# Loading the state-space decay rows on GpSimd's queue, with the first pair of each group taken out of the chain of side pieces

## The chip, the cores and the metric

The kernel runs on one core of a Trainium2 chip. The metric is the device time of one execution in microseconds (us), lower is better; several executions are taken and their median is compared. The engines are TensorE (PE, matmuls), VectorE (DVE), ScalarE (ACT), GpSimd (POOL) and SyncE (SP, which here only issues DMAs).

## The reference

One layer of a hybrid decoder trunk over 512 tokens of width 1024, in float32. A modulated RMSNorm gives h; one projection of h feeds three branches, whose gated sum goes through an output projection, and an MLP follows. The branch that the change touches is the state-space one (16 heads of 64 in two groups, chunks of 128 tokens). Cut to what matters:

```python
h = _rms(x, norm1_w) * (1 + sc1) + sh1
z, xbc, dt_raw, q, k, v, u, gates = split(h @ w_in)
xbc = silu(causal_dwconv(xbc, conv_w, conv_b))          # xs, B, C
a_cum = cumsum((dt * A) per chunk)
decay = exp(where(causal, a_cum[l] - a_cum[s], -inf))   # 128x128 per chunk and head
cb = einsum('bclgn,bcsgn->bclsg', C, B)
y_diag = einsum('bclgsj,bcsgjp->bclgjp', cb * decay, X) # X = xs * dt
states = einsum(B, X * exp(a_cum[last] - a_cum));  prev = scan over the chunks
y = y_diag + (C . prev) * exp(a_cum) + D * xs
y = rms_per_group(y * silu(z)) * ssd_norm_w;   y_ssd = y @ w_ssd_out
y_attn = dilated window attention @ w_attn_out
y_pool = (multi-scale pooling of u, mixed) @ w_pool_out
x = x + g1 * ((g_ssd*y_ssd + g_attn*y_attn + g_pool*y_pool) @ w_out)
x = x + g2 * (square(relu(h2 @ w_ff1)) @ w_ff2)         # h2: second modulated norm
```

## The kernel before

All activations lie with channels on 128 partitions and the 512 tokens along the row. Each float32 product is made of three matmuls over a high and a low part (mm3: lines L294, L295 and L296 of the profile are its three calls). A generator, wstream, streams weights: for each pair of 128-row blocks SyncE loads a 512 KB tile raw, ScalarE copies it to the high part wh (L279), VectorE subtracts for the low part wl (L280), and 24 matmuls follow. gemm_feat runs such a stream of 4 pairs into four PSUM banks psacc.

PSUM has 8 banks, and SBUF has 49 slots of 128x512 that all small tensors share (blk). Both are handed out first in, first out: a tensor takes the slot that was freed longest ago, whatever it held. So the first matmul into a new accumulator waits for the last reader of the tensor that had that bank before; and a load waits in the same way for the last user of its slot.

The state-space branch is side work. It is cut into pieces that wait in a list, side; after every weight pair tick() runs the next piece, and after every second one also a background piece that dots a 512-wide row block of the adaLN weights on VectorE (wa, L246, with its load). A scheduler then orders the instructions of each engine. The order of pieces for a group g of 8 heads is written in the main sequence: ssd_states(g) (transposes, cb L870, X L882, states, prev L895 and L897/L898), then do_heads(g), which drives four generators ssd_heads(g, j), one for each pair of heads:

- stage 1 loads two rows of prow, broadcast to 128 partitions, as the tiles M (256 KB each);
- stage 2 makes e = exp(-M) (ACT L917), relu(M - a) in four blocks on VectorE (L924) or ScalarE (L922), exp (ACT L925) and the product with cb (DVE L926);
- stage 3 does the matmuls psy (L932) and psyo (L940), adds them to conv (L935, L941, L943) and multiplies by z (L946).

Piece j of do_heads runs stage 1 of pair j+2, stage 2 of pair j+1 and stage 3 of pair j. ssd_scale and ssd_norm (psrr, diag L221, L959, split L322) follow. The main sequence around them is: x and z of group 0 (GEMMs xs0, z0), of group 1 (xs1, z1), then the gates and projections of the attention branch (GA0, its projection, GA1, its projection, in which L751 multiplies the projection by the gate sg), two pooling GEMMs U0 and U1 (windows L976 to L982 on VectorE, then four pooling mixes, psmix, whose weights wmix are split by L279 and L280 too and whose results are written by L1000), and the gate GS0 of the state-space branch.

Of the kernel before, what the change touches and what calls it, by code (L numbers as in the profile page):

```python
# [17 lines left out]
P = 128  # L18
D = 1024
T = 512  # L20
# [78 lines left out]
def kernel(ctx: ExitStack, tc: tile.TileContext, a: dict, out: bass.AP, dbg=None):  # L99
    nc = tc.nc  # L100
# [16 lines left out]
    class Slots:  # L117
# [12 lines left out]
        def free(self, t):  # L130
            self.idle.append(self.used.pop(id(t))[0])
# [3 lines left out]
    def blk(name, dt=F32):  # L135
        return sb.take(name, dt)
# [15 lines left out]
    def psm(name="m"):  # L152
        return banks.take("ps" + name, F32)
# [4 lines left out]
    def show(name, ap):  # L158
        if dbg is not None:
            dbg(name, ap)  # L160
# [64 lines left out]
    def add_square(sums, x):  # L225
        if sums is None:
            sums = blk("sums")
            S.activation(sums, x, AF.Square)
        else:
            sq = blk("sq")  # L230
            S.activation(sq, x, AF.Square)
            V.tensor_tensor(sums, sums, sq, ALU.add)
            free(sq)
        return sums
# [26 lines left out]
    side, ticks = [], [0]  # L261
# [508 lines left out]
    st = {}  # L770
# [132 lines left out]

    def ssd_heads(g, j, xs, z):

        X, prev, cb, CT = st[g]
        pc, npc, prow = st["pc"], st["npc"], st["prow"]

        Ms = [blk("M") for _ in range(2)]
        for half in range(2):  # L910
            hd = g * 8 + 2 * j + half
            nc.sync.dma_start(Ms[half], prow[hd : hd + 1, :].broadcast_to([P, T]))
        yield
        e = blk("e")
        for half in range(2):
            hd, M, fs = g * 8 + 2 * j + half, Ms[half], slice(64 * half, 64 * half + 64)
            S.activation(e[fs, P:], M[fs, P:], AF.Exp, scale=-1.0)  # L917
            for c in range(4):
                cs = slice(c * P, (c + 1) * P)
                hc = slice(c * 16 + hd, c * 16 + hd + 1)  # L920
                if half:
                    S.activation(M[:, cs], M[:, cs], AF.Relu, bias=npc[:, hc])  # L922
                else:
                    V.tensor_scalar(M[:, cs], M[:, cs], pc[:, hc], 0.0, ALU.subtract, ALU.max)  # L924
            S.activation(M, M, AF.Exp, scale=-1.0)  # L925
            V.tensor_tensor(M, M, cb, ALU.mult)  # L926
        yield
        yp = psm("y")
        for c in range(4):
            cs = slice(c * P, (c + 1) * P)  # L930
            for half in range(2):
                mm(yp[half * 64 : half * 64 + 64, cs], lhsT=X[c][:, (2 * j + half) * 64 : (2 * j + half + 1) * 64], rhs=Ms[half][:, cs], start=True, stop=True)  # L932
        free(*Ms)
        y = xs[j]
        V.scalar_tensor_tensor(y, xs[j], dcol[:, 4 * g + j : 4 * g + j + 1], yp, ALU.mult, ALU.add)  # L935
        free(yp)
        op = psm("yo")
        for c in range(3):
            cs = slice((c + 1) * P, (c + 2) * P)
            mm(op[:, cs], lhsT=prev[c][:, j * P : (j + 1) * P], rhs=CT[:, cs], start=True, stop=True)  # L940
        V.tensor_tensor(e[:, P:], op[:, P:], e[:, P:], ALU.mult)  # L941
        free(op)
        V.tensor_tensor(y[:, P:], y[:, P:], e[:, P:], ALU.add)  # L943
        show(f"y{g}{j}", y)
        free(e)
        V.tensor_tensor(y, y, z[j], ALU.mult)  # L946
        free(z[j])
        if j == 3:
            free(*X, *prev, cb, CT)
        st["sums", g] = add_square(st.get(("sums", g)), y)  # L950
# [66 lines left out]
    def call(f, *args):  # L1017
        side.append(lambda: f(*args))
# [22 lines left out]
    def rest(n):  # L1041
        side.extend([lambda: None] * n)

    def do_heads(g, xs, z):

        gens = [ssd_heads(g, j, xs, z) for j in range(4)]
        side.append(lambda: next(gens[0]))
        for j in range(-1, 4):
            def go(j=j):
                for i in (j + 2, j + 1, j):  # L1050
                    if 0 <= i < 4:
                        next(gens[i], None)
            side.append(go)
        rest(1)
        call(ssd_scale, g)
        call(ssd_norm, g, xs)
# [29 lines left out]
    do(ssd_states(0, xs0, BC), 6)  # L1086
    z0 = take_z(0)
    do_heads(0, xs0, z0)
    xs1 = take_x(1)
    z1 = take_z(1)  # L1090
    do(ssd_states(1, xs1, BC), 6)
    sg = gate(GA, 0)
    do_heads(1, xs1, z1)
    project(a["w_attn_out"], 4, 0, oh, ol, sg, first=True)
    sg = gate(GA, 1)
# [388 lines left out]
```

## Time and the profile before

| | before |
|---|---|
| median of 3 runs | 1095.87 us (1095.17 to 1096.69) |
| profiled execution, its own time | 1098.25 us |
| its span in the trace | 1096.5 us |
| TensorE busy | 1087.1 us |
| VectorE busy | 717.4 us |
| ScalarE busy | 527.8 us |
| GpSimd busy | 3.6 us |
| granted TensorE clock | 1.00 |

The span is the time from the first to the last instruction of the trace; the execution's own time is 1.75 us longer. Rows below show start and duration in us from the span's start, and in square brackets how long the engine stood idle just before, and what ended that.

### The profile page before, as it was taken

To read this page: it belongs to the slowest core of one execution; us is meant where nothing else is said; L and a number is where in the kernel's file an instruction comes from. 1 tells how busy PE (TensorE), PEld (TensorE's weight loads), DVE (VectorE), ACT (ScalarE), POOL (GpSimd) and SP (SyncE) were. 2 spreads that over 40 slices of the span, in tenths; PEclk is the share of its full clock that TensorE was granted. 3 is DMA by queue.
4 is the path that set the end of the run, shared out by engine and by line. 5 is a ranking of instruction groups with operands and counts; after the bars stand their busy time and mean duration, and the time that the engine had idled before them with its cause. 6 is when DMAs were issued, how large, how long until landed. Compare 5 with 4: busy or idle time off the path is not lost.

```text
span 1096.5 us, 14976 instructions
## 1 busy us (share of the span) xinstructions
PE 1087.1 (99%) x5806; PEld 927.0 (85%) x5806; DVE 717.4 (65%) x1383; ACT 527.8 (48%) x845; POOL 3.6 (0%) x10
## 2 busy tenths in 40 slices
PE   9999999999999999999999999999999999999998
PEld 7878888888887877888888888899889989989987
DVE  8975874582776778568843424577787587686664
ACT  8965875543695536625432123354344334335330
POOL 0000000000000000000000000000000000000000
PEclk9999999999999999999999999999999999999999
DMA  9853342443542354321232325360214224134032
GB/s 349 306 183 98 128 134 86 152 168 102 173 125 87 117 181 136 104 97 58 96 115 97 106 96 163 97 230 1 79 57 154 65 90 136 59 114 135 20 116 77
DMA packets 46666, 133.98 MB, mean 122 GB/s; under 512 B 5362, under 2 KB 6130, under 8 KB 46596
## 3 DMA queue, kind: packets, MB, share of 16 engines
q1 hardware_dynamic: 45392, 130.28, 36.0%
q0 software_dynamic: 480, 1.57, 0.5%
q10 hardware_dynamic: 724, 1.18, 0.3%
q8 instruction: 45, 0.74, 0.3%
q14 instruction: 25, 0.20, 0.1%
HBM read 130.89 MB, written 2.13 MB: 121 GB/s over the span
## 4 chain that ended last, share of the span: by engine, by line
PE 87%; ACT 4%; DVE 3%; DMA 3%; issue 1%; SPq 0%; ACTq 0%; DVEq 0%
PE psacc L294 22%; PE psacc L296 22%; PE psacc L295 22%; PE psacc L1345 11%; PE psacc L534 4%; DMA M<-prow 2%; PE psS L613 1%; DMA wa<-in_w_ada_dram 1%; DVE conv L850 1%; ACT wh L279 1%; PE pso L729 1%; PE pso L727 1%; DVE wl L280 1%; PE pskT L597 0%; PE psqT L592 0%
## 5 line engine op out<-in xcount | busy, mean ns | idle before, releaser
L280 DVE TENSOR_TENSOR wl<-raw,wh 128x1024 fp32r<-128x1024 f32 x140 | 171.0, 1222 | 192.2 <-ACT wh L279 190.9
L279 ACT CAST wh<-raw 128x1024 fp32r<-128x1024 f32 x140 | 146.8, 1050 | 241.1 <-PE psacc L295 168.8
L294 PE MATMUL psacc<-hl,wh 128*128 128x512 f32 x416 | 166.6, 401 | 3.4 <-DVE X L882 2.2
L295 PE MATMUL psacc<-hh,wh 128*128 128x512 f32 x416 | 162.1, 390 | 0.0
L296 PE MATMUL psacc<-hh,wl 128*128 128x512 f32 x416 | 162.0, 390 | 0.0
L295 PE MATMUL psacc<-ah,wh 128*128 128x512 f32 (+1 forms) x260 | 100.4, 386 | 0.0
L294 PE MATMUL psacc<-al,wh 128*128 128x512 f32 (+1 forms) x260 | 100.4, 386 | 0.0
L296 PE MATMUL psacc<-ah,wl 128*128 128x512 f32 (+1 forms) x260 | 100.3, 386 | 0.0
L294 PEld LDWEIGHTS psacc<-hl,wh 128*128 128x128 f32 x416 | 78.2, 188 | 21.7 <-DVE X L882 2.7
L295 PEld LDWEIGHTS psacc<-hh,wh 128*128 128x128 f32 x416 | 78.2, 188 | 16.9 <-issue 1.4
L296 PEld LDWEIGHTS psacc<-hh,wl 128*128 128x128 f32 x416 | 78.1, 188 | 16.7
L294 PE MATMUL psacc<-wl,rh 128*128 128x512 f32 x192 | 76.9, 401 | 0.0
L296 PE MATMUL psacc<-wh,rl 128*128 128x512 f32 x192 | 75.5, 393 | 0.0
L295 PE MATMUL psacc<-wh,rh 128*128 128x512 f32 x192 | 75.3, 392 | 0.0
L296 PEld LDWEIGHTS psacc<-ah,wl 128*128 128x128 f32 x260 | 48.8, 188 | 9.9
L294 PEld LDWEIGHTS psacc<-al,wh 128*128 128x128 f32 x260 | 48.9, 188 | 9.7
L295 PEld LDWEIGHTS psacc<-ah,wh 128*128 128x128 f32 x260 | 48.9, 188 | 9.6
L1405 DVE SCALAR_TENSOR_TENSOR xr<-psacc,modv,xr 128x512 f32<-128x512 f32 (+1 forms) x65 | 44.7, 739 | 18.6 <-PE psacc L296 18.6
L246 DVE SCALAR_TENSOR_TENSOR wa<-wa,crow 128x512 f32<-128x512 f32 x64 | 43.1, 688 | 20.0 <-DMA wa<-in_w_ada_dram 20.0
L296 PEld LDWEIGHTS psacc<-wh,rl 128*128 128x128 f32 x192 | 36.0, 188 | 7.6
L294 PEld LDWEIGHTS psacc<-wl,rh 128*128 128x128 f32 x192 | 36.1, 188 | 7.3 <-ACT qT L593 0.2
L295 PEld LDWEIGHTS psacc<-wh,rh 128*128 128x128 f32 x192 | 36.1, 188 | 7.0
(408 smaller groups left out, 2360.8 us busy)
## 6 DMA issues: line engine op xcount, KB each, us to landing
raw<-in_w_in_dram SPq DMA_DIRECT2D x80, 512.0 KB, 3.5
raw<-in_w_ff_dram SPq DMA_DIRECT2D x52, 512.0 KB, 3.7
wa<-in_w_ada_dram SPq DMA_DIRECT2D x64, 256.0 KB, 3.6
wada<-in_w_ada_dram SPq DMA_DIRECT2D x14, 512.0 KB, 7.8
rawl<-in_w_ff_dram SPq DMA_DIRECT2D x12, 512.0 KB, 3.5
wst<-in_w_in_dram SPq DMA_DIRECT2D x16, 256.0 KB, 7.8
M<-prow SPq DMA_DIRECT2D x16, 256.0 KB, 3.8
raw<-in_w_ssd_out_dram SPq DMA_DIRECT2D x8, 512.0 KB, 3.5
```

The source lines that it names most:

```text
L246: V.scalar_tensor_tensor(wa[i], wa[i], 1.0, crow[i], ALU.mult, ALU.mult, accum_out=d[:, i : i + 1])
L279: S.copy(wh, raw)
L280: V.tensor_tensor(wl, raw, wh.bitcast(F32), ALU.subtract)
L294: mm(ps, lhsT=wh, rhs=xl, start=first, stop=False)
L295: mm(ps, lhsT=wh, rhs=xh, start=False, stop=False)
L296: mm(ps, lhsT=wl, rhs=xh, start=False, stop=last)
L534: mm(ps[j], lhsT=t[:, j, :], rhs=w, start=first, stop=last)
L613: mm(so[b], lhsT=qT[:, b * P : (b + 1) * P], rhs=kT[:, (b + 1) * P - n : (b + 1) * P], start=True, stop=True)
L727: mm(od, lhsT=vs[kb][:, hs], rhs=pT[b // 2][:, cs : cs + P], start=(b == 0), stop=False, skip_group_check=True)
L729: mm(ov[:, b, :], lhsT=vs[b][:, hs], rhs=pT[0][:, b * P : (b + 1) * P], start=False, stop=(gi == 2 and b == 3), skip_group_check=True)
L1345: mm(o, lhsT=x[:, cs], rhs=y, start=first and k == 0 and j == 0 and n == 0, stop=k == 3 and n == 2, skip_group_check=True)
L1405: V.scalar_tensor_tensor(xT[d][:, ts], p[:, : ts.stop - ts.start], modv[:, 3, d : d + 1], xT[d][:, ts], ALU.mult, ALU.add)
```

## The change

The two loads of M go to GpSimd's queue, the look-up of the group's states moves behind the first yield, and do_heads makes the loads of the first pair at once instead of as a side piece of its own.

```diff
     def ssd_heads(g, j, xs, z):
 
-        X, prev, cb, CT = st[g]
         pc, npc, prow = st["pc"], st["npc"], st["prow"]
 
         Ms = [blk("M") for _ in range(2)]
         for half in range(2):
             hd = g * 8 + 2 * j + half
-            nc.sync.dma_start(Ms[half], prow[hd : hd + 1, :].broadcast_to([P, T]))
+            nc.gpsimd.dma_start(Ms[half], prow[hd : hd + 1, :].broadcast_to([P, T]))
         yield
+        X, prev, cb, CT = st[g]
         e = blk("e")
...
         gens = [ssd_heads(g, j, xs, z) for j in range(4)]
-        side.append(lambda: next(gens[0]))
+        next(gens[0])
         for j in range(-1, 4):
```

Each engine keeps its work, but much of it changes place. Numbers at the end of a name tell one tensor from another and differ between the two kernels.

VectorE at the beginning of the gate GA0. wl are weight splits, conv_3013, conv_3019 and conv_3025 the outputs of head pairs 1, 2 and 3 of group 0, wa the adaLN dots. Before:

```order
L246 SCALAR_TENSOR_TENSOR wa_3905,dot_3909<-wa_3905,crow_81 128x512
L246 SCALAR_TENSOR_TENSOR wa_3906,dot_3909<-wa_3906,crow_81 128x512
L248 TENSOR_TENSOR modv_94<-dot_3909 128x1
L280 TENSOR_TENSOR wl_3798<-raw_3795,wh_3797 128x1024
L935 SCALAR_TENSOR_TENSOR conv_3019<-conv_3019,dcol_93,psy_3665 128x512
L941 TENSOR_TENSOR e_3585<-psyo_3675,e_3585 128x384
```

Now:

```order
L246 SCALAR_TENSOR_TENSOR wa_3920,dot_3923<-wa_3920,crow_81 128x512
L946 TENSOR_TENSOR conv_3019<-conv_3019,z_3211 128x512
L248 TENSOR_TENSOR modv_94<-dot_3923 128x1
L256 TENSOR_TENSOR modv_94<-modv_94,vec_79 128x1
L232 TENSOR_TENSOR sums_3510<-sums_3510,sq_3652 128x512
L924 TENSOR_SCALAR M_4268<-M_4268,pc_947 128x128
L280 TENSOR_TENSOR wl_3815<-raw_3812,wh_3814 128x1024
L935 SCALAR_TENSOR_TENSOR conv_3025<-conv_3025,dcol_93,psy_3685 128x512
L941 TENSOR_TENSOR e_3620<-psyo_3695,e_3620 128x384
```

Head pair 3 stands where pair 2 stood, and an L924 on an M row of group 1 has moved ahead of the weight split and of L935.

VectorE from cb of group 1 to the X that a bank of the gate GA1 waits for. Before:

```order
L870 TENSOR_TENSOR cb_3957<-pscb_3964,cst 128x512
L924 TENSOR_SCALAR M_4245<-M_4245,pc_947 128x128
L926 TENSOR_TENSOR M_4413<-M_4413,cb_3957 128x512
L924 TENSOR_SCALAR M_4279<-M_4279,pc_947 128x128
L924 TENSOR_SCALAR M_4245<-M_4245,pc_947 128x128 x2
L751 TENSOR_TENSOR sg_3914<-psacc_3922,sg_3914 128x512
L751 TENSOR_TENSOR sg_3915<-psacc_3923,sg_3915 128x512
L751 TENSOR_TENSOR sg_3916<-psacc_3924,sg_3916 128x512
L751 TENSOR_TENSOR sg_3917<-psacc_3925,sg_3917 128x512
L882 TENSOR_TENSOR X_4005<-psX_4000,dt_885 128x512
```

Now, the last twelve rows of this stretch (ahead of them stand cb, two wa products, two splits L322, four L926 and a tiny one):

```order
L882 TENSOR_TENSOR X_3979<-psX_3974,dt_885 128x512
L280 TENSOR_TENSOR wl_4090<-raw_4087,wh_4089 128x1024
L887 TENSOR_TENSOR Xd_3981<-X_3979,dst_950 128x512
L256 TENSOR_TENSOR modv_94<-modv_94,vec_79 128x1
L926 TENSOR_TENSOR M_4268<-M_4268,cb_3906 128x512
L246 SCALAR_TENSOR_TENSOR wa_4376,dot_4379<-wa_4376,crow_81 128x512
L751 TENSOR_TENSOR sg_3928<-psacc_3940,sg_3928 128x512
L751 TENSOR_TENSOR sg_3929<-psacc_3941,sg_3929 128x512
L751 TENSOR_TENSOR sg_3930<-psacc_3942,sg_3930 128x512
L751 TENSOR_TENSOR sg_3931<-psacc_3943,sg_3931 128x512
L280 TENSOR_TENSOR wl_4141<-raw_4138,wh_4140 128x1024
L897 TENSOR_TENSOR prev_4084<-prev_4024,dec_949 128x512
```

The next row is L882 of X_4018, which the bank waits for. The L924 on freshly loaded rows have left the stretch (they run earlier), and X of the first chunk stands a whole weight pair earlier.

VectorE in the gate GS0, around the split of a mixing weight wmix. Before:

```order
L976 COPY win_4868<-win_4865 128x2
L977 TENSOR_TENSOR win_4868<-win_4865 128x510
L981 TENSOR_TENSOR win_4856<-win_4856,cst 128x15
L280 TENSOR_TENSOR wl_4950<-wmix_4947,wh_4949 128x512
L280 TENSOR_TENSOR wl_4978<-raw_4975,wh_4977 128x1024
```

Now:

```order
L976 COPY win_4902<-win_4899 128x8
L977 TENSOR_TENSOR win_4902<-win_4899 128x504
L981 TENSOR_TENSOR win_4884<-win_4884,cst 128x15
L280 TENSOR_TENSOR wl_4948<-wmix_4945,wh_4947 128x512
L280 TENSOR_TENSOR wl_4976<-raw_4973,wh_4975 128x1024
```

The split that stood here belonged to mix 0 and now belongs to mix 1 (mix 0 is done at the end of U1). Ahead of it the windows of U1 have gone further (win_4902 at 8 tokens where win_4868 stood at 2), and two L1000 of mix 0 stand among them.

## Rows read from the trace of the kernel before

**Rows 1.** The page: span, and busy us (share) of each engine.

```profile
span 1096.5 us, 14976 instructions
...
PE 1087.1 (99%) x5806; PEld 927.0 (85%) x5806; DVE 717.4 (65%) x1383; ACT 527.8 (48%) x845; POOL 3.6 (0%) x10
```

**Rows 2.** Waits of TensorE: who for whom, total us, times, longest.

```profile
PE psacc L294 <- DVE X L882: 2.2, 1, 2.2
...
PE psacc L294 <- DVE conv L935: 0.5, 1, 0.5
PE psacc L294 <- ACT prev L895: 0.5, 1, 0.5
```

**Rows 3.** TensorE's timeline at three places: start, us, instruction, idle before.

```profile
336.81 0.50 PE L294 MATMUL psacc<-hl,wh 128*128 128x512 f32 x1 [0.50 <-ACT prev L895]
...
388.90 0.50 PE L294 MATMUL psacc<-hl,wh 128*128 128x512 f32 x1 [0.51 <-DVE conv L935]
...
431.01 0.50 PE L294 MATMUL psacc<-hl,wh 128*128 128x512 f32 x1 [2.22 <-DVE X L882]
431.35 0.40 PE L295 MATMUL psacc<-hh,wh 128*128 128x512 f32 x1
431.58 0.39 PE L296 MATMUL psacc<-hh,wl 128*128 128x512 f32 x1
```

**Rows 4.** VectorE's timeline ahead of the third place.

```profile
422.34 0.68 DVE L870 TENSOR_TENSOR cb<-pscb,cst 128x512 f32<-128x512 f32 x1
...
427.29 0.68 DVE L924 TENSOR_SCALAR M<-M,pc 128x128 f32<-128x128 f32 x3 [2.92 <-DMA M<-prow]
427.88 2.48 DVE L751 TENSOR_TENSOR sg<-psacc,sg 128x512 f32<-128x512 f32 x4
430.27 0.68 DVE L882 TENSOR_TENSOR X<-psX,dt 128x512 f32<-128x512 f32 x1
```

**Rows 5.** The chain that ended last, in order of time: start, us, link.

```profile
311.42 3.30 DMA M<-prow
...
420.13 3.87 DMA M<-prow
```

**Rows 6.** SyncE's timeline: DMA issues ahead of the third place.

```profile
419.53 2.20 SPq L912 DMA_DIRECT2D M<-prow  x3
```

**Rows 7.** The page's DMA issues: engine, count, KB each, median us to landing.

```profile
M<-prow SPq DMA_DIRECT2D x16, 256.0 KB, 3.8
...
al<-in_const_dram POOLq DMA_DIRECT2D x4, 256.0 KB, 3.3
...
toNat<-in_const_dram POOLq DMA_DIRECT2D x1, 256.0 KB, 4.2
toMod<-in_const_dram POOLq DMA_DIRECT2D x1, 256.0 KB, 4.3
```

**Rows 8.** Tile al, last line of its view.

```profile
DMA to landing us min/median/max: 2.9/3.3/4.7
```

**Rows 9.** Tile M, last line of its view.

```profile
DMA to landing us min/median/max: 3.1/3.8/6.5
```

**Rows 10.** VectorE's timeline at the start of GA0 (starts give the pitch).

```profile
386.96 1.23 DVE L280 TENSOR_TENSOR wl<-raw,wh 128x1024 fp32r<-128x1024 f32 x1
388.10 0.74 DVE L935 SCALAR_TENSOR_TENSOR conv<-conv,dcol,psy 128x512 f32<-128x512 f32 x1
388.76 0.55 DVE L941 TENSOR_TENSOR e<-psyo,e 128x384 f32<-128x384 f32 x1
```

**Rows 11.** VectorE's timeline in GS0: windows, then a weight split.

```profile
527.70 0.15 DVE L976 COPY win<-u 128x1 f32<-128x1 f32 x1
527.76 0.68 DVE L977 TENSOR_TENSOR win<-u 128x511 f32<-128x511 f32 x1
528.36 0.68 DVE L322 TENSOR_TENSOR pdl<-win,pdh 128x512 fp32r<-128x512 f32 x1
...
530.38 0.69 DVE L280 TENSOR_TENSOR wl<-wmix,wh 128x512 fp32r<-128x512 f32 x1
```

## Prediction

> **What bounds the kernel now.** I read the page's busy times first: TensorE works 1087.1 of 1096.5 us and VectorE 717.4 [rows 1]. So the end is set by TensorE's stream of matmuls, and a change that adds and removes no matmul can win or lose only in the 9.4 us in which TensorE does not work. I then read the view of waits for TensorE alone. Of those 9.4 us it puts 2.2 us to X (L882), 0.5 us to conv (L935) and 0.5 us to prev (L895) [rows 2]; these three are the ones that belong to the state-space branch. No row of it names a weight split (L279, L280) or a weight load, so the streamed weights arrive early enough everywhere today. The timeline of TensorE places the three: 336.81 us (A, start of the x GEMM of group 1, behind prev), 388.90 us (C, start of the gate GA0), 431.01 us (B, start of the gate GA1) [rows 3]. In each a GEMM begins, its four accumulators need four free PSUM banks, and the bank it asks for is still being read by side work. Together: 0.50 + 0.51 + 2.22 = 3.2 us, 0.3% of the time. That is all the change can give back here.
>
> Then I asked what is late ahead of each. At B VectorE itself stood still for 2.92 us, waiting for a row of M, and only then did the four L751 (2.48 us) and X (L882) follow [rows 4]; the chain of waits has that load, 3.87 us long from 420.13 [rows 5]. SyncE issued three M rows there in one go, 2.20 us long [rows 6]. At A the chain has another M load, 3.30 us from 311.42 [rows 5], and from its landing to prev VectorE (conv, L850) and ScalarE (table loads, exponentials, z) are busy nearly without a gap, so prev moves with that landing.
>
> **The change part by part.** It removes no arithmetic. 16 loads of M leave SyncE's queue for GpSimd's; one side piece of each group vanishes, so the pieces of group 0 come one tick (a weight pair: 24 matmuls, 24 x 0.23 = 5.5 us by the pitch in [rows 3]) earlier and those of group 1 two.
>
> *SyncE's queue.* 16 issues less. The weight loads behind them may start up to 2.2 us earlier [rows 6], and no wait of TensorE is on them: worth nothing.
>
> *The loads on GpSimd.* The trace does not show M on that queue. Nearest rows: six other 256 KB loads from GpSimd land in 3.3 (al, median of four, 2.9 to 4.7), 4.2 and 4.3 us [rows 7, 8]; M from SyncE in 3.8 (3.1 to 6.5) [rows 7, 9]. Lower bound 2.9, upper bound 6.5 (M's own worst). I take 3.7, between 3.3 and 4.2. GpSimd does nothing else, so issuing waits for nothing but the buffer.
>
> *A.* The second pair's buffer comes free at the same moment as before, so the load starts at about 311.4. It took 3.30 us; with 3.7 the stall grows from 0.50 to about 0.9. Bounds: 0.1 (landing 2.9) and 3.7 (6.5).
>
> *C.* Before, L935 of head pair 2 stood on this place. Now pair 3 is the last ahead of GA0, and VectorE has, ahead of its L935, an L924 on the row M_4268 of group 1 (shown in the section on the change). That buffer is freed by the product of wa_3920, about 384.6 us by counting 0.6 us for each 512-wide operation. So: 384.6 + 3.3 (al's median) = 387.9, L924 0.2, L280 1.14, L935 0.66 [rows 10] = 389.9; TensorE asks for the bank six matmuls after the start of GA0, also at 389.8. I take 3.7 for the landing: 0.5 us, as much as now. Bounds 0 and 3.3 (6.5).
>
> *B.* The M rows of group 1 are now loaded some 25 us ahead of use, so the 2.92 us go. But VectorE's work does not: from cb (about 413.8 us) to the X that TensorE asks for (X_4018) stand 14.2 us of instructions (eleven 512-wide at 0.6, two weight splits at 1.14, three products of wa at 0.67, four L751 in 2.48, X 0.68, two small ones at 0.1): 428.0. TensorE's own clock, matmuls counted at 0.23: GA0 from 388.8, 96 matmuls 21.8, the norm and cb 2.5, so 413.1 (hence cb on VectorE at 413.8); the projection's 48 matmuls 10.9, X and a state 1.3, so GA1 at 425.3. It asks for the bank nine matmuls later, at 427.4, or 427.9 with small waits on the way. Add half a microsecond for waits on ScalarE's exponentials that I can't place: stall 0.9 us, in place of 2.22. Bounds 0.2 and 1.7. **Gain 1.3.**
>
> *Side work that moved to places where there is none now.* The y blocks of group 1 stand in the attention projection and in U0, its norm in U1, where by the same counting conv and diag come within 0.3 us of the moment they are asked for: 0.2 us for both together, bounds 0 and 2. I leave the hand-offs of group 0's norm at what they cost today.
>
> *F, new.* The first two mixing pieces move forward: gi 0 to the end of U1, gi 1 into the second weight pair of GS0. In front of gi 1's weight split wl_4948 VectorE now has 37 operations of the pooling windows: 20 512-wide at 0.60 and 17 tiny at 0.07 [rows 11], 12.0 + 1.2 + 0.1 = 13.3, and the split itself 0.6. They can begin when the first accumulator of U1 has been copied out, 1.4 us before U1 ends, so wl_4948 is ready at U1's end + 12.5. TensorE asks for it after gi 0 (12 matmuls, 2.7), a pair of GS0 (5.5) and 12 more (2.7): end + 10.9. **Loss 1.6 us** (bounds 0, if TensorE arrives that much later for a cause that I don't see, and 3, if the operations begin only when U1 has ended). In the kernel before the corresponding split ran at 530.38 and nothing waited.
>
> *Sum.* After: A 0.9 + C 0.5 + B 0.9 + 0.2 + F 1.6 = 4.1. Before: 3.2. Net +0.9 us. The profiled execution took 1098.25 (span 1096.5 and 1.75 around it), 2.4 above the median of the runs shown. 1098.25 + 0.9 = 1099.1 there, and on the median's footing 1095.87 + 0.9 = **1096.8 us**. A measurement of this kernel can tell about 0.2%, 2.2 us, from no change, so this is "no difference".
>
> A rule of the Trainium skill speaks against the change. Its page SBUF — State Buffer, section "SBUF: two separate sides", says that a DMA issued by GpSimd has its descriptors written by GpSimd's cores, which are locked out of SBUF while VectorE runs certain single-source copies and scalar operations. By that rule a row of M can land late by one such operation; here these are L924 and L976, which [rows 11] and the order show as short ones, so it would make A and C later by some 0.3 us each, and the sum 1097.4 rather than 1096.8. No run so far shows M on that queue.
>
> **Rivals.** *1. All three waits go and nothing new comes.* Speaks for it: B's cause is plainly M [rows 4]. Against: at A the load is as late as before, and at F VectorE has 13.9 us of work in 12.3. Time: 1095.87 - 3.2 = 1092.7. Chance 9%.
>
> *2. Slower: a row of M lands late on GpSimd's queue.* The mechanism sits at A and C, where no work lies between landing and TensorE that could be left out, so each microsecond of later landing costs two. At 3.7 us the net is +0.9; it passes +2.2 at 3.7 + 1.3 / 2 = 4.4 us. al's worst, 4.7 [rows 8], gives +2.9, 1098.8; M's worst, 6.5 [rows 9], +6.5, 1102.4. For it: GpSimd's single loads at 4.2 and 4.3 stand just below that point. Against: al's median 3.3. Chance 22%. (The rule above is one way to it.)
>
> *3. The change does nothing*, since TensorE is at 99% and the stalls move elsewhere one for one: 1095.9. Chance 10%.
>
> *4. F alone turns out at 3 us*: +2.3, 1098.2. Chance 4%.
>
> **How the numbers follow.** The forecast holds 55%; its own range, from the bounds that are near (A 0.5 to 1.3, C 0 to 1, B 0.2 to 1.7, F 0.9 to 2.5), is 1095.0 to 1098.0. The range for 8 in 10 leaves out rival 1 and the far end of rival 2 (landing above 5.2 us): 1094.2 to 1099.8. Faster by over 0.2% (below 1093.7): rival 1, 8%. Slower by over 0.2% (above 1098.1): rivals 2 and 4, 26%. Within: 66%.
>
> **What would show it.** Right: TensorE's wait for X at GA1 below 1.7 us, VectorE with no wait for M there, M landing near 3.7 us, TensorE standing at the second pair of GS0 for wl (L280), prev still waited for at the start of group 1's x. Wrong: no wait in GS0; or waits for prev and conv of 2 us and more, with M landing above 4.4; or a new wait at a place that I counted as covered.

## The result, and the profile of the changed kernel

| | before | changed |
|---|---|---|
| median | 1095.91 us (6 runs) | 1103.97 us (6 runs) |
| range | 1095.17 to 1096.69 | 1101.46 to 1105.47 |
| profiled execution, its span | 1098.25, 1096.5 | 1104.54, 1102.8 |

The ratio is 1.0072, 95% interval [1.0059, 1.0086]: the change makes the kernel 8 us slower. The forecast was 1096.8, no difference, with 1099.8 as its upper end.

The page's first lines, which answer to [rows 1]:

```profile
span 1102.8 us, 14975 instructions
...
PE 1089.5 (99%) x5806; PEld 928.4 (84%) x5806; DVE 715.6 (65%) x1383; ACT 523.5 (47%) x842; POOL 12.1 (1%) x26
```

TensorE runs the same 5806 matmuls, yet is busy 2.4 us longer, and stands still 13.3 us instead of 9.4. So there are two things to look for: longer waits, and matmuls that ran slower. The view of TensorE's waits, which answers to [rows 2]:

```profile
PE psacc L294 <- DVE o L737: 2.6, 1, 2.6
PE psmix L296 <- DVE wl L280: 1.7, 1, 1.7
PE psacc L294 <- ACT prev L895: 1.6, 1, 1.6
PE pssx L412 <- DVE sq L421: 1.2, 1, 1.2
PE pswarm L405 <- DVE ones L374: 1.1, 1, 1.1
PE psacc L294 <- DVE cb L870: 0.6, 1, 0.6
PE psrr L222 <- DVE diag L221: 0.4, 1, 0.4
PE psrx L466 <- DVE diag L463: 0.3, 1, 0.3
PE psacc L294 <- DVE conv L935: 0.2, 1, 0.2
```

The wait for X is gone, and so is that for conv at GA0 (the 0.2 us for conv here stand in U0); the wait for prev has trebled, and two big ones are new. The wait for wl is F of the prediction. The one for o, in the attention branch, the prediction does not have at all. TensorE's timeline places the three:

```profile
294.20 0.50 PE L294 MATMUL psacc<-hl,wh 128*128 128x512 f32 x1 [2.61 <-DVE o L737]
...
342.85 0.50 PE L294 MATMUL psacc<-hl,wh 128*128 128x512 f32 x1 [1.62 <-ACT prev L895]
...
536.07 0.50 PE L296 MATMUL psmix<-pdh,wl 128*128 128x512 f32 x1 [1.65 <-DVE wl L280]
```

**The wait for o**, followed back through three timelines. ScalarE:

```profile
279.06 0.40 ACT L922 ACTIVATE M<-M,npc 128x128 f32<-128x128 f32 x1 [6.62 <-DMA M<-prow]
279.37 1.03 ACT L279 CAST wh<-raw 128x1024 fp32r<-128x1024 f32 x1
...
291.02 1.28 ACT L852 ACT_TABLE_LOAD   x1 [3.05 <-DVE conv L850]
292.32 0.63 ACT L852 ACTIVATE conv<-conv 128x512 f32<-128x512 f32 x1
292.86 0.57 ACT L736 CAST o<-pso 128x512 fp32r<-128x512 f32 x1
```

SyncE's queue:

```profile
281.69 0.33 SPq L287 DMA_DIRECT2D raw<-in_w_in_dram  x1
282.06 7.10 SPq L240 DMA_DIRECT2D wa<-in_w_ada_dram  x5
```

VectorE:

```profile
280.43 1.23 DVE L280 TENSOR_TENSOR wl<-raw,wh 128x1024 fp32r<-128x1024 f32 x1 [3.09 <-ACT wh L279]
...
286.11 0.69 DVE L246 SCALAR_TENSOR_TENSOR wa<-wa,crow 128x512 f32<-128x512 f32 x1 [3.85 <-DMA wa<-in_w_ada_dram]
...
293.45 0.69 DVE L737 TENSOR_TENSOR o<-pso,o 128x512 fp32r<-128x512 f32 x1 [1.18 <-ACT o L736]
```

Read it forwards. One M row of group 0 is loaded early, and the first quarter of its relu (L922) now stands in ScalarE's order just ahead of a weight split. ScalarE waits 6.62 us for the row, so the split (L279, then L280) is late. Its raw tile therefore comes free late, and the next raw load stands in SyncE's queue waiting for that tile, at 281.69; the wa loads are behind it and go out from 282.06 on. VectorE waits 3.85 us for wa, with conv (L850) queued behind; ScalarE's L852 waits for conv, with o (L736) queued behind; VectorE's L737 needs that, and the bank that it reads is the one that TensorE wants. ScalarE, VectorE, SyncE, VectorE, ScalarE and VectorE once more lie between the row of M and TensorE, and nearly every link is in-order work behind a waiting instruction.

**The wait for prev**: the chain that ended last has the load, which was 3.30 us long in [rows 5]:

```profile
316.57 4.21 DMA M<-prow
```

**The slower matmuls**: the windows of the first microseconds (TensorE busy, ..., granted clock as the third number from the end):

```profile
8.00:10.00 2.00, 1.29 (x10) 1.29 (x11) 1.90 (x4) 1.88 (x4) 0.00 (x0) 0.91 1.05 351
10.00:12.00 2.00, 2.00 (x11) 2.00 (x11) 1.90 (x3) 1.97 (x3) 0.00 (x0) 0.50 1.02 373
12.00:14.00 2.00, 2.00 (x16) 2.00 (x15) 0.95 (x6) 0.00 (x0) 0.00 (x0) 0.74 1.01 372
```

After the 1.15 us in which TensorE waits for sq, the granted clock fell from 1.00 to 0.50 (from 2.4 to 1.2 GHz) and stayed there for about 3 us. In before that wait was 0.92 us, in experiment 8, the same kernel once more, 1.18 us, and the clock stayed at 1.00 in both.

### The profile page after: what moved, and what is told of

Same layout as the page of the kernel before. It is cut to its first block, busy times and chain, and to the rows that moved or that the text cites. A ratio compares the mean times of both kernels' runs of the same rounds, so it can differ in the third digit from the quotient of the medians.

```text
span 1102.8 us, 14975 instructions
## 1 busy us (share of the span) xinstructions
PE 1089.5 (99%) x5806; PEld 928.4 (84%) x5806; DVE 715.6 (65%) x1383; ACT 523.5 (47%) x842; POOL 12.1 (1%) x26
## 3 DMA queue, kind: packets, MB, share of 16 engines
q10 hardware_dynamic: 724, 1.18, 0.3%
## 4 chain that ended last, share of the span: by engine, by line
PE 64%; DVE 3%; ACT 3%; DMA 1%; issue 1%; ACTq 0%; DVEq 0%
PE psacc L294 17%; PE psacc L296 17%; PE psacc L295 17%; PE psacc L1345 11%; DVE win L977 1%; DVE wl L280 1%; ACT wh L279 1%; PE psy L932 1%; DMA raw<-in_w_in_dram 1%; DVE conv L850 1%; PE psyo L940 0%; PE psst L891 0%; DMA M<-prow 0%; ACT L917 0%; ACT e L917 0%
## 5 line engine op out<-in xcount | busy, mean ns | idle before, releaser
L280 DVE TENSOR_TENSOR wl<-raw,wh 128x1024 fp32r<-128x1024 f32 x140 | 170.8, 1221 | 198.8 <-ACT wh L279 197.4
L279 ACT CAST wh<-raw 128x1024 fp32r<-128x1024 f32 x140 | 146.7, 1049 | 243.7 <-PE psacc L295 175.8
```

Source lines behind the costliest of these rows:

```text
L279: S.copy(wh, raw)
L280: V.tensor_tensor(wl, raw, wh.bitcast(F32), ALU.subtract)
```

## The experiments

Times are medians; each ratio, with its interval, is against runs of the kernel before on the same chip. Experiments 1 to 4 shared a median of before of 1095.93, 5 to 8 of 1096.41, 9 and 10 of 1096.51, 11 of 1095.82.

**1. The order of the change, the loads on SyncE.**

```diff
-            nc.gpsimd.dma_start(Ms[half], ...)
+            nc.sync.dma_start(Ms[half], ...)
```

> The changed order with the M loads left on SyncE's queue. Theory (order and queue each cost something, by the profile after): TensorE's wait for o (L737) near 294 us stays at about 2.5 us, since the relu L922 of an early M row still stands ahead of a weight split on ScalarE; the wait for wl in GS0 stays at about 1.6; the wait for prev goes back from 1.6 to about 0.5, since the load lands in about 3.3 us again; no fall of the granted clock at the start. Sum against before: +2.5 +1.6 +0.6 (cb) +0.5 -2.7 (X, conv) = about +2.5 us, 1098.4. Rival (the whole loss is GpSimd's queue): the time of before or up to 2.7 us faster, 1093 to 1096.

Measured: 1098.07, ratio 1.0013 [1.0003, 1.0024]. TensorE waits 1.65 us for wl and 1.20 for o; there is no wait for prev, X or conv. TensorE's order is word for word that of the changed kernel. So wl belongs to the order alone, and o to both: on SyncE the early row still holds ScalarE up (5.32 us, ending at 275.45), but it arrives earlier relative to the rest: it lands 13.9 us before TensorE begins to wait for o, and 12.6 us before it in the changed kernel. My 2.5 for o was too high.

**2. The order of before, all M loads on GpSimd.**

```diff
-            nc.sync.dma_start(Ms[half], ...)
+            nc.gpsimd.dma_start(Ms[half], ...)
```

> The order of before with the M loads on GpSimd's queue. Theory: no wait for o near 294 us and none for wl in GS0; prev waits about 1.5 us instead of 0.5 and X about 3 instead of 2.2, by a landing of 4.2 instead of 3.3 us: +1.8 us, about 1097.7, plus about 2 us in runs whose granted clock falls in the first 20 us, if GpSimd's queue is what brings that. Rival (the whole loss is the queue's): about 1103 to 1104 with waits for M that reach TensorE at several places.

Measured: 1102.37, ratio 1.0048 [1.0032, 1.0065]. The queue costs 5.3 us by the ratio and 6.4 by the medians, not 2; that is nearer to the rival. The order of experiment 1 costs 1.4 and 2.1 in the same way. TensorE's order is that of before; VectorE's and ScalarE's differ from it in a few places. TensorE's waits:

```profile
PE psacc L294 <- DVE X L882: 2.1, 2, 1.9
PE psrr L222 <- DVE diag L221: 1.7, 1, 1.7
PE pssx L412 <- DVE sq L421: 1.7, 1, 1.7
PE psacc L294 <- ACT prev L895: 1.5, 1, 1.5
```

No wait for o and none for wl, as expected; prev as expected; X waits 1.9 us and not 3. The wait for diag, at the norm of group 0, I had not foreseen. Experiment 11 takes it up.

**3. The changed kernel, group 0's first pair a side piece again.**

```diff
-        next(gens[0])
+        if g == 0:
+            side.append(lambda: next(gens[0]))
+        else:
+            next(gens[0])
```

> The changed kernel, but group 0 keeps its first pair's load as a side piece; only group 1's is out of the chain. Theory: the wait for o (2.6 us) is gone, since no relu of M stands ahead of the weight split there; the mixes move one tick and not two; prev still waits 1.6. About 2.6 us under the changed kernel, more if the wait for wl in GS0 goes too: 1099.5 to 1101.5. Rival (the wait for o comes from the wa loads on SyncE's queue or from a shift in time, not from M's row): the wait stays, 1103 to 1104.

Measured: 1098.26, ratio 1.0018 [1.0009, 1.0028]. The waits for o and wl are gone, prev waits 1.51, X and diag do not wait. It is faster than forecast, and by 4 us faster than experiment 2, from which its source differs only in the move of group 1. So that move is a gain of about 4 us when the rows come from GpSimd.

**4. The changed kernel, the first mixes two ticks later.**

```diff
-        rest(2)
+        rest(2 if half else 4)
```

> The changed kernel with two empty side pieces more ahead of the first mixes. Theory: the wait for wl in GS0 (1.65 us) goes or shrinks below 0.5, the rest is as in the changed kernel: 1.2 to 1.7 us faster than it, about 1102.5. Rival (the same work on VectorE makes TensorE wait wherever the mixes stand): no change, 1104.

Measured: 1101.30, ratio 1.0039 [1.0025, 1.0052]; the wait for wl is gone. The medians, from different sessions, differ by 2.7 us and not by 1.65; where the last microsecond comes from was not settled. In its profile the clock falls at another place, right behind the wait for o (2.70 us, ending at 292.20):

```profile
292.00:294.00 2.00, 1.80 (x7) 1.42 (x8) 1.98 (x5) 1.98 (x4) 0.00 (x0) 0.83 0.91 328
294.00:296.00 2.00, 2.00 (x6) 1.61 (x5) 2.00 (x4) 1.95 (x4) 0.00 (x0) 0.50 0.18 64
```

**5. Experiment 3 with all loads on SyncE**: group 1's first pair out of the chain, nothing else changed against before.

```diff
-            nc.gpsimd.dma_start(Ms[half], ...)
+            nc.sync.dma_start(Ms[half], ...)
```

> All M loads on SyncE; group 0's first pair stays a side piece, only group 1's is out of the chain (the third experiment without its queue). Theory (the queue costs at prev, the move of group 0 costs at o, the move of group 1 is what gains): no wait for o, none for wl in GS0, prev 0 to 0.5 instead of 1.5, X and conv near 0: 1 to 2.5 us under the third experiment's 1098.3 and level with before or up to 2 us faster, 1094 to 1096.5. Rival (GpSimd's queue does the gaining at the gate GA1, by keeping three M issues off SyncE's queue): the wait for X comes back, 1097 or more.

Measured: 1095.55, ratio 0.9987 [0.9978, 0.9996]. TensorE waits 0.34 us for conv, 0.19 for prev, and not for X, o or wl. It beats before by about 1 us; under 0.2%, but its interval leaves out 1. It has the lowest median of all versions here, 0.2 us below experiment 7.

**6. Before, with one pair's two loads on GpSimd.**

```diff
-            nc.sync.dma_start(Ms[half], ...)
+            (nc.gpsimd if (g, j) == (0, 2) else nc.sync).dma_start(Ms[half], ...)
```

> The kernel before with only the two M rows of head pair 2 of group 0 on GpSimd's queue; every engine's order is that of before but for these two. Theory (a load from GpSimd lands about 0.9 us later at that place, 4.2 instead of 3.3, and nothing lies between it and TensorE): prev waits 1.3 to 1.6 instead of 0.5 or less, and the time is 1 to 1.5 us more than before, 2 more in runs where the clock then falls: 1096.5 to 1099. Rival (GpSimd's queue costs only when all 16 loads are on it, by waiting in line): no change, 1095.9.

Measured: 1097.43, ratio 1.0011 [1.0003, 1.0020], and the wait for prev is 1.50 us. TensorE, VectorE and ScalarE have the order of before row for row, so this is the price of the pair's two loads on GpSimd by themselves. The load in the chain that ended last, and VectorE behind it:

```profile
311.89 4.19 DMA M<-prow
```

```profile
311.18 1.22 DVE L280 TENSOR_TENSOR wl<-raw,wh 128x1024 fp32r<-128x1024 f32 x1
316.18 0.29 DVE L924 TENSOR_SCALAR M<-M,pc 128x128 f32<-128x128 f32 x1 [3.78 <-DMA M<-prow]
```

VectorE was idle through the last 3.78 us of it. A load of the same row by SyncE took 3.54 us (experiment 8) or 3.30 ([rows 5]). The landing is not all of the delay. The end of ScalarE's copy L331 frees the row's buffer; then come the load of the row and the next weight load. Here, and below it in experiment 8, where SyncE loads the row:

```profile
310.71 0.59 ACT L331 COPY xc<-psacc 128x512 f32<-128x512 f32 x1
...
311.89 0.54 POOL L912 DMA_DIRECT2D M<-prow  x1 [120.69 <-ACT xc L331]
...
312.43 0.33 SPq L287 DMA_DIRECT2D raw<-in_w_in_dram  x1
```

```profile
311.42 0.59 ACT L331 COPY xc<-psacc 128x512 f32<-128x512 f32 x1
...
312.04 0.33 SPq L912 DMA_DIRECT2D M<-prow  x1
...
313.14 0.33 SPq L287 DMA_DIRECT2D raw<-in_w_in_dram  x1
```

GpSimd begins the load 0.59 us after the buffer is free (0.48 to 0.49 in the changed kernel and in experiments 2, 3, 4 and 9), SyncE 0.03 (0.02 to 0.04 in the seven profiles in which it loads this row). And the weight load goes out 0.54 us behind the row here and 1.10 there. Over all profiles, GpSimd's loads of M land in 4.08 to 4.58 us where a weight load is the only load that goes out from 1 us ahead of the row to 2 us behind it and follows by 0.5 to 0.75 us (18 loads), and in 3.27 to 3.55 where it follows by 1.25 us or more (7 loads). So the longer landing goes with the weight load close behind it; no run sets that gap by itself.

**7. Experiment 5 with group 1's loads on GpSimd.**

```diff
-            nc.sync.dma_start(Ms[half], ...)
+            (nc.gpsimd if g else nc.sync).dma_start(Ms[half], ...)
```

> As the fifth experiment, with group 1's eight loads on GpSimd and group 0's on SyncE. Theory (a later landing costs nothing where the row is loaded ahead of use): within 1 us of the fifth experiment, prev at 0 to 0.5, about 1095 to 1096.5. Rival (the queue costs wherever it is used): 2 us or more above the fifth.

Measured: 1095.78, ratio 0.9990 [0.9981, 0.9999], 0.2 us from experiment 5. Where a row is loaded ahead of use, GpSimd's queue costs nothing that these runs can tell.

**8. Before once more.** No edit; one more profile of the same kernel.

> The kernel before, unchanged, profiled once more. Theory: the waits for X, conv and prev are there again within 0.5 us each. Rival: the profiled execution, 2.4 us above the median, was an unusual one, and the wait for X (2.2 us) is much smaller in a common one; then the gain that the changed order could bring at that place was overrated.

Measured: 1096.82, span 1095.0. TensorE's waits:

```profile
PE psacc L294 <- DVE conv L935: 0.8, 1, 0.8
PE psacc L294 <- ACT prev L895: 0.5, 1, 0.5
```

X is not among them. VectorE's timeline at [rows 4] says why:

```profile
425.82 0.68 DVE L924 TENSOR_SCALAR M<-M,pc 128x128 f32<-128x128 f32 x3 [0.35 <-DMA M<-prow]
```

The row of M came 0.35 us late here and 2.92 us late in [rows 4]. So the rival holds: the wait of 2.22 us on which the gain at B rested was that of one execution, and not of a common one. In the two other profiles that have before's order and SyncE's loads at this place, the wait is 0 (here) and 0.32 us (experiment 6).

**9. The changed kernel, the halves of a pair exchanged.**

```diff
-                if half:
+                if not half:
                     S.activation(M[:, cs], ...)
```

> The changed kernel with the two halves of a head pair changing engines for the relu: half 0 on ScalarE, half 1 on VectorE. The early M row of group 0 then holds up VectorE in front of the weight split's second half (L280) and no longer ScalarE in front of its first (L279); TensorE's order is that of the changed kernel. Theory (M's row delays the split, the split delays the raw load on SyncE, that the wa loads behind it, these conv and o): the split ends when M has landed plus 1.3 us and not plus 2.6, so the wait for o shrinks from 2.6 to 1.2 to 1.6; about 1 us faster than the changed kernel, 1101 to 1103. Rival (the wait for o comes from the wa loads' own places or from slots, not from the row ahead of the split): it stays at 2.4 or more.

Measured: 1100.01, ratio 1.0034 [1.0022, 1.0045]. VectorE, and then TensorE:

```profile
278.33 0.29 DVE L924 TENSOR_SCALAR M<-M,pc 128x128 f32<-128x128 f32 x1 [1.95 <-DMA M<-prow]
278.54 1.22 DVE L280 TENSOR_TENSOR wl<-raw,wh 128x1024 fp32r<-128x1024 f32 x1
```

```profile
292.25 0.50 PE L294 MATMUL psacc<-hl,wh 128*128 128x512 f32 x1 [1.46 <-DVE o L737]
```

The early row now stands ahead of the split's second half, which ends 1.4 us behind the row and not 2.6, and the wait for o falls from 2.61 to 1.46, inside the forecast. That shows the link from the row to o. The total fell by more than that, since the wait for prev went too, which I had not expected. In VectorE's timeline no L924 on the row loaded at 314.59 stands ahead of conv any more, so conv does not wait for it:

```profile
316.81 2.78 DVE L850 SCALAR_TENSOR_TENSOR conv<-xc,vec,conv 128x511 f32<-128x511 f32 x4 [1.61 <-ACT conv L848]
```

The GpSimd load at A costs TensorE only because in-order work stands behind its first reader.

**10. Experiment 5 with seven more warm-up calls (14 matmuls in the trace) at the wait for sq.**

```diff
-WARM = (7, 2, 8, 5, 7)
+WARM = (7, 9, 8, 5, 7)
```

> The fifth experiment with 9 instead of 2 warm-up matmuls in the place where TensorE waits about 1.1 us for sq (L421) at 8 us. Theory (the granted clock falls to half now and then after a wait of TensorE of some 1 us or more, and costs about 2 us each time): the wait at 8 us shrinks to 0.1 to 0.4, no run has a mean clock of 0.998 or less, the median is that of the fifth experiment's undisturbed executions, 1095 to 1095.6, and no run lies above 1097. Rival (the fall has nothing to do with the wait): one run in five or six still falls to 0.998 and 1097 or more.

Measured: 1096.21, ratio 1.0005 [0.9995, 1.0015]. The wait for sq is gone from the profile, but one of 12 runs still has a mean clock of 0.998 (1101.04 us) and four lie above 1097. A wait of 1.32 us for pT is in its profile, and the clock stays at 1.00 behind it. So filling the wait for sq does not do away with the falls; theory and rival both miss. It is no gain.

**11. Before, group 1's eight loads on GpSimd** (experiment 7 without the move).

```diff
-            nc.sync.dma_start(Ms[half], ...)
+            (nc.gpsimd if g else nc.sync).dma_start(Ms[half], ...)
```

> The kernel before, every engine's order as there, with only group 1's eight M loads on GpSimd's queue (the seventh experiment without the move of group 1). Theory (a row that is used as soon as it lands costs TensorE its later landing, a row loaded ahead of use costs nothing): the wait for diag (L221) at the norm of group 0 and that for X at the gate GA1 come up as in the second experiment, about 1.7 and 1.9 us, prev stays at 0.5: 2.5 to 3.5 us above before, and 2 more where the clock then falls: 1099 to 1101. Rival (the second experiment's loss came mostly from group 0's loads, or from all sixteen in one queue): within 1 us of before, 1096.5.

Measured: 1099.42, ratio 1.0030 [1.0020, 1.0040]; TensorE's and ScalarE's orders are those of before, and VectorE's is as far as the wait for diag. The size was right, the places half: diag waits 1.82 us, X only 0.19. The load, the wait, and the granted clock behind it:

```profile
406.00 4.58 DMA M<-prow
```

```profile
416.20 0.71 PE L222 MATMUL psrr<-diag,ones 128*128 128x128 f32 x4 [1.82 <-DVE diag L221]
```

```profile
416.00:418.00 2.00, 1.80 (x10) 1.57 (x10) 0.85 (x4) 1.97 (x3) 0.00 (x0) 0.78 0.61 229
418.00:420.00 2.00, 2.00 (x7) 1.61 (x6) 1.57 (x3) 1.99 (x4) 0.00 (x0) 0.50 0.00 0
```

In before a relu on VectorE (L924) of a row of group 1 stands among the small steps of group 0's norm; it waits for the row, and diag is queued behind it. With the loads of experiment 7 out of the chain the same rows on the same queue cost nothing. The medians of the two differ by 3.6 us. With SyncE's loads the same move gains 0.9 us (experiment 5), so some 3 us of it are the price of using a row from GpSimd as soon as it lands.

## Why the prediction was wrong

The sum said +0.9 us and the kernel lost 8. Term by term:

- **F, the mixes: right.** Predicted 1.6, measured 1.65 in the changed kernel and in experiment 1, gone in experiment 4. Both sides of the sum came out too: VectorE's work up to wl took 14.1 us (counted 13.9), and TensorE began to wait 11.2 us after U1's end (counted 10.9).
- **A, prev: right place, too small.** I took a landing of 3.7 us; it was 4.21 here and 4.13 to 4.28 in experiments 2, 3, 4 and 6. And I let the load start when its buffer comes free, where GpSimd began it 0.49 us later. Predicted 0.9, measured 1.62. The median of the al loads [rows 7, 8] misled me; the other two GpSimd loads of [rows 7], 4.2 and 4.3 us, lay nearer. This was rival 2's mechanism, and experiment 6 measures it alone: +1.0 us.
- **C: no wait was left** where I had 0.5; the row landed in 3.42 us there. A wait of 0.21 came up at U0, and the norm of group 0, which I had left at today's cost, waited 0.40 for diag.
- **B: what is left was overrated, and what is won even more.** Predicted 0.9 of a wait for X; measured 0, but 0.55 for cb came up one GEMM earlier, in the attention projection. But the 2.22 us to be won were in one profile, and not in experiment 8. The profiled execution stood 2.4 us above the median; I noted the difference and drew nothing from it.
- **The step that failed** is that on SyncE's queue and on group 0: "no wait of TensorE is on them: worth nothing", with nothing set down for the pieces of group 0, which by the prediction "come one tick" earlier. The early load of group 0 was moved ahead of a weight split on ScalarE, and through the split, the raw load and the wa loads, TensorE was reached 15 us later: 2.61 us. The wait is there in the changed kernel and in experiments 1, 4 and 9, which move group 0's piece, and in none of the others; experiment 9 moves it in size by moving one link. Taking back group 0's move alone (experiment 3) takes 5.7 of the 8 us away: the waits for o, wl, cb and diag go with it.
- **What a wait costs was missing.** I priced a wait at its length. The granted clock fell to 0.50 right behind a wait of TensorE in five profiles: the changed kernel (8 us), experiments 2 (338 us, behind prev), 4 (292 us, behind o), 5 (9 us, behind sq) and 11 (twice). It does not follow every wait, nor the longest: in the changed kernel it fell behind the 1.15 us for sq and not behind the 2.61 for o, and it stayed at 1.00 behind 2.22 us for X in before and 1.50 for prev in experiment 6. The runs' mean clocks say how often. At 0.998 or less, as a profile with one fall shows it, were 5 of 6 runs of the changed kernel and 5 of 7 of experiment 4 (both wait over 2.5 us for o), 6 of 15 of experiments 2 and 11 (waits near 1.8), 8 of 74 of the other experiments, and 9 of 82 of before. Within before, runs with the fall have a median of 1098.71, the others of 1096.09: 2.6 us for the wait and the fall together. The one run of the changed kernel without a fall took 1101.46 us, the other five 1102.92 to 1105.47. That longer waits bring more frequent falls is a count over different kernels, not an experiment that sets the wait; experiment 10, the attempt at one, did not settle it, and what decides whether a wait brings a fall stays open.

The account of the 8 us, against the profile of experiment 8 (span 1095.0, TensorE 1087.1 busy): the span is 7.8 us longer, 5.4 of it idle (o 2.6, wl 1.65, prev 1.1, cb 0.55, diag 0.4, conv -0.6, small ones -0.3 to -0.5) and 2.4 in slower matmuls. By experiments 1 and 2 the order is 0.13% of it and the queue 0.48%; together 0.61%, beside 0.72% [0.59, 0.86] for both at once. That the two add up is in part luck. With GpSimd's loads the move of group 1 gains 4 us and that of group 0 costs 5.7 (experiments 2 and 3 and the changed kernel); with SyncE's it is 0.9 and 2.5 (experiments 5 and 1, from different sessions).

The rule of the Trainium skill that I weighed (the page SBUF — State Buffer, section "SBUF: two separate sides": a DMA from GpSimd is held up while VectorE runs certain single-source copies and scalar operations) pointed the right way, but no run shows it at work. In experiment 6 VectorE ran the two-source subtraction L280 for the first 0.51 us of the load and then stood idle, 3.78 us, until the row was there. What the rows show there is GpSimd's later start and the weight load that goes out closer behind the row. Whether that closeness is the whole of the 0.6 to 0.9 us by which the landing is longer was not tested.

## What to carry to other kernels

A load that is used the moment it lands sets a price on every microsecond of its queue; first load it ahead of use (experiments 5 and 7 gain, on either queue), and only then ask which queue; another queue also changes which loads go out side by side. When a side piece moves, look in each engine's order for what its first waiting instruction now stands ahead of, and follow that through the queues, the DMA queues too, until it ends; an early piece did the most harm here. And check a stall in a second profile before counting it as something to win: a profiled execution above the median can have stalls that a common one has not.

## What the hardware showed that I had not expected

- At the same place of the kernel, with the buffer free, SyncE began the 256 KB broadcast load of a row after 0.02 to 0.04 us and GpSimd after 0.48 to 0.59. It landed in 3.30 and 3.54 us from SyncE and in 4.13 to 4.29 from GpSimd, with the next weight load 1.10 us behind it in the one case and 0.54 to 0.64 in the other.
- The granted clock fell from 1.00 to 0.50 (2.4 to 1.2 GHz) behind single waits of TensorE between 1.1 and 2.7 us, and not behind others of the same lengths. It came back after 3 to 4 us in five of the six falls in the profiles and after nearly 7 in the sixth (experiment 11).
